# An mLSTM stage in one written order on all engines: block ends, stores, weights and roots placed a counted number of products later

## The chip, the cores and the metric

The kernel runs on one NeuronCore of a Trainium2 chip. Its time is the device time of one execution in microseconds. Three runs of the kernel before gave 2363.53 us at the median (2361.35 to 2365.49).

## The reference: what is computed

One encoder layer over 2048 tokens of width 1024, in float32. What bears on this case is the mLSTM half of the mixer, which works chunk by chunk (16 chunks of 128 tokens) for each of four heads, forward and backward in time:

```python
proj = hmix @ w_in                              # q_a, k_a, v_a, q_m, k_m, v_m, o_m, gates
qk = jax.nn.silu(centred_dwconv(jnp.concatenate([q_m, k_m], axis=-1), conv_w, conv_b))
kv_c = jnp.einsum('bchs,bchsk,bchsv->bchkv', w, kc, vc)
c_new = decay * c_st + inj * kv                 # one state per chunk, scanned over the chunks
sc = jnp.einsum('bchtd,bchsd->bchts', qc, kc) * dw
num = jnp.einsum('bchts,bchsv->bchtv', sc, vc) + inter * jnp.einsum('bchtk,bchkv->bchtv', qc, c_prev)
hout = num / jnp.maximum(jnp.abs(den), jnp.exp(-m_t))
h_m = rms_norm(h_fwd + h_bwd, g_mlstm_out)
```

The other half is banded attention (its query and key projections are made in the same stretch), followed by the output projection and a SwiGLU FFN. The output must have the reference's values to float32 accuracy; products are made of three passes with a high and a low part of each operand (`hi*hi`, `hi*lo`, `lo*hi`).

## The kernel before

The layer's input, normalised and transposed, lies in SBUF as four `hT` tiles of 512 tokens, each as a high and a low part. A projection column block of 128 columns is made by `proj_mm` (L421 to L426): for each block of 512 tokens, 8 x 3 = 24 matmuls of 128x512 (called products here) go into one PSUM bank `gps`, of which there are two. A column block is thus 4 x 24 = 96 products. Two kinds of code use it:

- `conv_tile` (L428) makes q or k of one mLSTM head: after each 24 products ACT copies the bank with the middle tap (`cacc`, L452), fixes the edges between blocks (L453 to L456), DVE adds the two side taps (L457, L458), and `finish` (L436) makes the silu of the previous block by a tanh on ACT (L439) and a product on DVE (L440), then stores it to DRAM (`qk_d`, L442).
- `qk_att` (L467) makes attention's queries and keys: a high part on ACT (`qhi`, L483), a low part on DVE (`qlo`, L484), four or eight stores.

`mlstm(h, nb, nf, last)` (L535) runs one head. Backward pass (L572 to L587): per chunk a transpose of k (`ktp`) to `kn`, `vw = w*v` on ACT, then one chunk later the matmul `kvp` and DVE's update of the state table `cb`. Forward pass (L593 to L673): `scores(cc)` makes the decay matrix `ng` (POOL L606, then two exponentials on ACT L609), `qs` (POOL L611), the matmul `sps` and DVE's `sc` (L615); one chunk later `products` makes `kvp`, the state `cf` (DVE L629), the four matmuls of `num` (L634, L636), and DVE's chain `den`, `rd`, `rd`, `rd`, `hst`, `hst` (L643 to L648), then a square with a sum on ACT (`mjk`, L650). After every fourth chunk `rsqrt` (L92) makes a root of 12 small DVE instructions and POOL scales `hst` (L653); `store` transposes it five chunks later.

Projection products fill the gaps: `fill` is a queue of generators, and `pull(n)` emits the next n products. A backward chunk pulls `nb` = 3 of them, a forward chunk `nf` = 8, and between heads 60 are pulled at once. A head therefore takes 45 + 127 products, and with the 60 between heads the projections of head h+1 are done before `mlstm(h+1)` starts.

What sets the order: PE is issued as the program is written (`tc.manual_schedule`, "hand") from here on. The other four engines' queues are in written order too ("win") during the first 252 products, where the gates are computed beside the projections of head 0; `win` is closed before `mlstm(0)`. In the mLSTM stage the order of DVE, ACT, POOL and SP is chosen by a scheduler when the program is built, from its own estimates of durations. Each engine then works through its queue in that fixed order, and one that waits holds up what stands behind it in the queue.

Loads: `load_qk` and `load_v` fetch the next block of four chunks at the block's second chunk; `load_bc` (four rows of decays, 256 KB as broadcast) is issued one chunk before its use. `proj_cols` loads and splits the weights of a column block (`whi` on ACT, `wlo` on POOL, L230, L231) when its generator begins.

Of the kernel before, what the change touches and what calls it, by code (L numbers as in the profile page):

```python
# [21 lines left out]
P = 128  # L22
# [7 lines left out]
HM = 4  # L30
# [6 lines left out]
def hybrid_layer_kernel(  # L37
# [196 lines left out]
    def proj_cols(c0):  # L234
        _, w = cols_steps(c0)
        return w
# [191 lines left out]
    def conv_tile(j, h, ws_=None):  # L428


        w = ws_[0] if ws_ else proj_cols((C_QM, C_KM)[j] + h * P)
# [5 lines left out]
        def finish(a, n):  # L437
            t = s2.tile([P, 512], F32, tag="ctanh", name="ctanh")
            act.activation(t, a, AF.Tanh)  # L439
            dve.scalar_tensor_tensor(a, t, 1.0, a, ADD, MUL)  # L440
            yield True
            sp.dma_start(qk_d[j, h, n], a)  # L442

        end = None
        for n in range(NB):
            ps = bank("g", "gps")
            for i, _ in enumerate(proj_mm(ps, w, n)):
                if end and i in (6, 14):
                    next(end, None)
                yield True  # L450
# [6 lines left out]
            dve.scalar_tensor_tensor(a[:, 1:], ps[:, :511], w0, a[:, 1:], MUL, ADD)  # L457
            dve.scalar_tensor_tensor(a[:, :511], ps[:, 1:], w2, a[:, :511], MUL, ADD)  # L458
# [5 lines left out]
        for f in (end, finish(prev, NB - 1)):  # L464
            deque(f, 0)

    def qk_att(pl, tags, j):  # L467

        w = proj_cols(C_QA + j * P)
        wait = deque()  # L470
        for n in range(NB):
            ps = bank("g", "gps")
            for i, _ in enumerate(proj_mm(ps, w, n)):
                if wait and i % 3 == 2:
                    sp.dma_start(*wait.popleft())
                yield True
            while wait:
                sp.dma_start(*wait.popleft())
# [5 lines left out]
            dve.scalar_tensor_tensor(lo, ps, s, hi.bitcast(F32), MUL, SUB)  # L484
            for i in range(2):
                rs = slice(i * 64, (i + 1) * 64)
                if j < 4:
                    wait.append((qst_d[2 * j + i, 0:64, ts], hi[rs].bitcast(F32)))
                    wait.append((qst_d[2 * j + i, 64:128, ts], lo[rs].bitcast(F32)))
                else:  # L490
                    for z in range(2):
                        wait.append((kst_d[i, 0, z * 64:(z + 1) * 64, ts], hi[rs].bitcast(F32)))
                        wait.append((kst_d[i, 1, z * 64:(z + 1) * 64, ts], lo[rs].bitcast(F32)))
        while wait:
            sp.dma_start(*wait.popleft())
# [39 lines left out]
    def mlstm(h, nb, nf, last):  # L535
# [28 lines left out]


# [3 lines left out]
        for cc in list(range(NT - 1, 0, -1)) + [0, 0]:  # L569
            tick()  # L570
            n, i = divmod(cc, 4)
            if i == 2 and n:  # L572
                blk[n - 1] = (load_qk(h, 1, n - 1), load_v(h, n - 1))
            if cc == 2:
                ahead = (load_qk(h, 0, 0), load_qk(h, 1, 0), load_v(h, 0)), load_bc(0)
# [3 lines left out]
            if len(todo) > 1 or (todo and not cc):  # L579
# [7 lines left out]
                pull(nb // 2)  # L587


        blk = {0: ahead[0]}  # L590
        out_ = {}
        bcs = {0: ahead[1]}
# [3 lines left out]
        def scores(cc):  # L596
            n, i = divmod(cc, 4)
            if cc + 1 < NT:
                bcs[cc + 1] = load_bc(cc + 1)
            if i == 2 and n + 1 < NB:  # L600
# [3 lines left out]
            bc = bcs.pop(cc)  # L604
            ng = s2.tile([P, 2, P], F32, tag="ng", name="ng")
            pool.tensor_tensor(ng, bc[:, 0:2, :], maskb, ADD)  # L606
            for d in range(2):
                rr = row(d, cc)
                act.activation(ng[:, d, :], ng[:, d, :], AF.Exp, bias=rT[:, rr:rr + 1])  # L609
# [1228 lines left out]
```

## Time and profile before

| what | time |
|---|---|
| median of three runs | 2363.53 us |
| the profiled execution | 2361.98 us |
| its span in the trace | 2360.2 us |
| PE busy in the span | 2258.3 us (96%) |
| first 252 products with the gates | about 201 to 264 us of the span |
| mLSTM stage, four heads | about 264 to 624 us |
| attention, output projection, FFN | from 624 us to the end |

Instants are microseconds from the span's start. A row of the timeline has the start, the duration, the engine, the line, the operation and what it writes and reads; in brackets the engine's idle time before it and what ended that. Matmuls overlap, so the time that one takes from the stream is the distance between two starts, not its duration. The table of windows gives busy time per engine in a stretch and the clock granted to TensorE as a share of full speed (PEclk).

### The profile page before, as it was taken

The numbers are of one execution on the slowest core, as the hardware profiler recorded it, in microseconds if no ns is written. First come the engines' busy times: TensorE is split into PE (matmuls) and PEld (weight loads), VectorE is DVE, ScalarE is ACT, GpSimd is POOL, SyncE is SP. The second block draws the span as 40 slices with busy tenths as digits, with TensorE's granted clock in tenths as the row PEclk, the third lists the DMA queues.
The fourth block names the chain that finished last, engine by engine and source line by source line (L and its number), as shares of the span: only waits on it lengthen the run. The fifth ranks groups of instructions, "written<-read, shape, count | busy, mean of one in ns | idle before, by whom it ended". The sixth has DMA issues, their size and how long they took to land.

```text
span 2360.2 us, 32454 instructions
## 1 busy us (share of the span) xinstructions
PE 2258.3 (96%) x10811; PEld 1873.2 (79%) x10811; DVE 1608.5 (68%) x2998; ACT 1061.6 (45%) x2205; POOL 1045.8 (44%) x876
## 2 busy tenths in 40 slices
PE   5998999999999999999999999899999999999998
PEld 4987777878888877777888878688888778888886
DVE  6777486676687887775656766766666645784684
ACT  3523455535487755443545434433333333233452
POOL 1004643344334433525656655465666654592020
PEclk9999999999999999999999999999999999999999
DMA  8565855477666666763343444432333273443452
GB/s 296 175 208 176 266 161 168 150 223 215 186 185 178 195 204 221 251 241 130 107 146 127 152 145 156 159 107 94 110 101 112 96 268 114 164 152 93 157 187 89
DMA packets 355515, 393.39 MB, mean 167 GB/s; under 512 B 21396, under 2 KB 253196, under 8 KB 355348
## 3 DMA queue, kind: packets, MB, share of 16 engines
q1 hardware_dynamic: 355348, 391.32, 51.4%
q8 instruction: 85, 1.39, 0.2%
q14 instruction: 82, 0.67, 0.1%
HBM read 272.06 MB, written 119.19 MB: 166 GB/s over the span
## 4 chain that ended last, share of the span: by engine, by line
PE 53%; DVE 2%; DMA 2%; issue 1%; ACT 1%; POOL 1%; SPq 0%; DVEq 0%; ACTq 0%; POOLq 0%
PE fp L56 11%; PE fp L57 11%; PE fp L58 11%; PE fo L58 6%; PE fo L56 6%; PE fo L57 6%; PE ops L56 1%; PE ops L58 1%; PE ops L57 1%; DMA al<-a_d 0%; DMA hop_d<-n 0%; DVE T L1331 0%; DMA B<-hop_d 0%; DMA a_d<-u 0%; PE trn L163 0%
## 5 line engine op out<-in xcount | busy, mean ns | idle before, releaser
L424 PE MATMUL gps<-hT,whi 128*128 128x512 f32 x1088 | 398.5, 420 | 0.0
L56 PE MATMUL fo<-w,ah 128*128 128x512 f32 x616 | 242.2, 393 | 2.6 <-ACT ah L1622 2.6
L58 PE MATMUL fo<-w,al 128*128 128x512 f32 x616 | 242.6, 394 | 0.5 <-DVE al L1623 0.5
L57 PE MATMUL fo<-w,ah 128*128 128x512 f32 x616 | 242.0, 393 | 0.0
L424 PE MATMUL gps<-hT,wlo 128*128 128x512 f32 x544 | 228.6, 420 | 0.0
L56 PE MATMUL fp<-T,S 128*128 128x512 f32 x528 | 209.4, 397 | 15.8 <-ACT u L1531 15.5
L424 PEld LDWEIGHTS gps<-hT,whi 128*128 128x128 f32 x1088 | 202.5, 191 | 24.5 <-DVE cacc L458 0.7
L57 PE MATMUL fp<-T,S 128*128 128x512 f32 x528 | 207.8, 394 | 0.8 <-DVE T L1331 0.8
L58 PE MATMUL fp<-T,S 128*128 128x512 f32 x528 | 207.5, 393 | 0.0
L1623 DVE TENSOR_TENSOR al<-al,ah 128x1024 fp32r<-128x1024 f32 x77 | 112.0, 1459 | 125.3 <-ACT ah L1622 125.1
L1366 DVE TENSOR_TENSOR A<-graw,A 128x512 fp32r<-128x512 f32 x86 | 95.7, 1119 | 123.4 <-ACT A L1365 123.2
L1366 DVE TENSOR_TENSOR S<-sf,S 128x512 fp32r<-128x512 f32 x86 | 130.1, 1551 | 59.6 <-ACT S L1365 59.5
L1622 ACT ACTIVATE ah<-al 128x1024 fp32r<-128x1024 f32 x77 | 81.6, 1060 | 189.9 <-DMA al<-a_d 189.8
L56 PEld LDWEIGHTS fo<-w,ah 128*128 128x128 f32 x616 | 116.0, 188 | 29.1 <-ACT ah L1622 3.1
L56 PE MATMUL fp<-B,A 128*128 128x512 f32 x352 | 138.1, 392 | 0.0
L58 PEld LDWEIGHTS fo<-w,al 128*128 128x128 f32 x616 | 115.9, 188 | 27.4 <-DVE al L1623 1.0
L57 PE MATMUL fp<-B,A 128*128 128x512 f32 x352 | 137.6, 391 | 0.0
L58 PE MATMUL fp<-B,A 128*128 128x512 f32 x352 | 137.6, 391 | 0.0
L57 PEld LDWEIGHTS fo<-w,ah 128*128 128x128 f32 x616 | 115.9, 188 | 26.5
L56 PEld LDWEIGHTS fp<-T,S 128*128 128x128 f32 x528 | 99.6, 189 | 40.1 <-ACT u L1531 18.1
L716 POOL TENSOR_SCALAR ap<-ap,adn 128x384 f32<-128x384 f32 (+1 forms) x128 | 73.1, 590 | 127.3 <-DVE adn L714 57.7
L1370 POOL TENSOR_TENSOR sf<-A,A22r 128x512 f32<-128x512 f32 x43 | 58.0, 1348 | 147.7 <-DMA A22r<-in_w_ffn_in_dram 116.8
(419 smaller groups left out, 6165.6 us busy)
## 6 DMA issues: line engine op xcount, KB each, us to landing
al<-a_d SPq DMA_DIRECT2D x77, 512.0 KB, 3.9
wmod<-in_w_mod_dram SPq DMA_DIRECT2D x48, 512.0 KB, 5.6
graw<-in_w_ffn_in_dram SPq DMA_DIRECT2D x43, 512.0 KB, 4.2
a_d<-ka SPq DMA_DIRECT2D x66, 256.0 KB, 4.7
bc<-bc_d SPq DMA_DIRECT2D x64, 256.0 KB, 3.7
hop_d<-n SPq DMA_DIRECT2D x56, 256.0 KB, 4.3
a_d<-u SPq DMA_DIRECT2D x55, 256.0 KB, 4.6
mqk<-qk_d SPq DMA_DIRECT2D x48, 256.0 KB, 4.1
```

What stands on the lines that cost most here:

```text
L56: pe.matmul(o, lh, rh, start=first, stop=False, skip_group_check=skip)
L57: pe.matmul(o, lh, rl, start=False, stop=False, skip_group_check=skip)
L58: pe.matmul(o, ll, rh, start=False, stop=last, skip_group_check=skip)
L424: pe.matmul(ps, w[i == 2][:, k, :], hT[n](i == 1, k), start=(k == 0 and i == 0), stop=(k == KT - 1 and i == 2))
L716: pool.tensor_scalar(self.p[g][:, :self.NK], self.p[g][:, :self.NK], dn[:, g:g + 1], 0.0, MUL, ADD)
L1366: dve.tensor_tensor(t[:, 1, :], f, t[:, 0, :].bitcast(F32), SUB)
L1370: pool.tensor_tensor(f1, a21, a22, ADD)
L1622: act.activation(ah, al.bitcast(F32), AF.Copy)
L1623: dve.tensor_tensor(al, al.bitcast(F32), ah.bitcast(F32), SUB)
```

## The change

All of it lies in the mLSTM stage. `put_soon(k, f, ...)` puts an instruction on a list, and `beat`, called after each product that `pull` emits, counts the list down and emits what is due. With it:

- a convolution block's side taps are emitted 4 products after its bank copy, the tanh 4 later, the silu product 4 after that, the store 5 later; `qlo` comes 4 products after `qhi`, the stores two products apart; the store of a normalised block 4 products after its copy; the root and POOL's scaling 5 products after the fourth chunk's square;
- weights of the next column block are loaded 6 products after the current one begins and split 48 products after (`next_cols`);
- the written order ("win") now holds for all five engines until the end of the mLSTM stage, so that no scheduler orders them there;
- loads move ahead: blocks of the backward pass at the block's first chunk, of the forward pass three chunks ahead instead of two, `bc` two chunks ahead instead of one, the next head's first block three chunks before the current head ends; block 0's keys and values, which the backward pass has loaded, are used again in the forward pass (8 loads fewer: 44 of `mqk` instead of 48, 28 of `mv` instead of 32);
- `ng` and its exponentials are made one chunk ahead (`prep`), behind `qs` of the current chunk;
- products are spread: `nb` = 4, `nf` = 10, and none between heads (60 + 159 products per head instead of 45 + 127 + 60).

No arithmetic is added or removed. The count of every instruction but the eight loads is the same, and outside the stage the order of the instructions on each engine is the same.

```diff
+    soon = []
+    def put_soon(k, f, *args):
+        soon.append([k, f, args])
+    def beat(k=1):
+        for e in soon:
+            e[0] -= k
+        due = [e for e in soon if e[0] <= 0]
+        soon[:] = [e for e in soon if e[0] > 0]
+        for _, f, args in sorted(due, key=lambda e: e[0]):
+            f(*args)
     def pull(n=1):
-        while n > 0 and fill:
-            if next(fill[0], None) is None:
+        while n > 0:
+            if not fill:
+                n -= 1
+                beat()
+            elif next(fill[0], None) is None:
                 fill.popleft()
             else:
                 n -= 1
+                beat()
...
+    ready, coming = deque(), deque()
+    def next_cols():
+        w = ready.popleft()
+        if coming and not ready:
+            g = cols_steps(coming.popleft())
+            put_soon(6, next, g)
+            put_soon(48, lambda: ready.append(next(g)))
         return w
...
+        def sides(a, ps):
+            dve.scalar_tensor_tensor(a[:, 1:], ps[:, :511], w0, a[:, 1:], MUL, ADD)
+            dve.scalar_tensor_tensor(a[:, :511], ps[:, 1:], w2, a[:, :511], MUL, ADD)
+        def finish(a, n, at):
             t = s2.tile([P, 512], F32, tag="ctanh", name="ctanh")
-            act.activation(t, a, AF.Tanh)
-            dve.scalar_tensor_tensor(a, t, 1.0, a, ADD, MUL)
-            yield True
-            sp.dma_start(qk_d[j, h, n], a)
+            put_soon(at, act.activation, t, a, AF.Tanh)
+            put_soon(at + 4, dve.scalar_tensor_tensor, a, t, 1.0, a, ADD, MUL)
+            put_soon(at + 9, sp.dma_start, qk_d[j, h, n], a)
...
-            dve.scalar_tensor_tensor(a[:, 1:], ps[:, :511], w0, a[:, 1:], MUL, ADD)
-            dve.scalar_tensor_tensor(a[:, :511], ps[:, 1:], w2, a[:, :511], MUL, ADD)
+            put_soon(4, sides, a, ps)
             if prev is not None:
-                end = finish(prev, n - 1)
-                if not ws_:
-                    deque(end, 0)
+                put_soon(7, finish, prev, n - 1, 1)
...
-            dve.scalar_tensor_tensor(lo, ps, s, hi.bitcast(F32), MUL, SUB)
+            put_soon(4, dve.scalar_tensor_tensor, lo, ps, s, hi.bitcast(F32), MUL, SUB)
...
+        def prep(cc):
+            ng = ngs[cc] = s2.tile([P, 2, P], F32, tag="ng", name="ng")
+            pool.tensor_tensor(ng, bcs[cc][:, 0:2, :], maskb, ADD)
+            for d in range(2):
+                rr = row(d, cc)
+                act.activation(ng[:, d, :], ng[:, d, :], AF.Exp, bias=rT[:, rr:rr + 1])
...
-            if i == 2 and n:
+            if i == 3 and n:
                 blk[n - 1] = (load_qk(h, 1, n - 1), load_v(h, n - 1))
             if cc == 2:
-                ahead = (load_qk(h, 0, 0), load_qk(h, 1, 0), load_v(h, 0)), load_bc(0)
+                q_first = load_qk(h, 0, 0)
+            if cc in (4, 2):
+                bcs[2 - cc // 2] = load_bc(2 - cc // 2)
...
-        blk = {0: ahead[0]}
+        blk = {0: (q_first, *blk[0])}
...
-            if cc + 1 < NT:
-                bcs[cc + 1] = load_bc(cc + 1)
-            if i == 2 and n + 1 < NB:
+            if cc + 2 < NT:
+                bcs[cc + 2] = load_bc(cc + 2)
+            if i == 1 and n + 1 < NB:
                 blk[n + 1] = (load_qk(h, 0, n + 1), load_qk(h, 1, n + 1), load_v(h, n + 1))
...
             if i == 3:
-                r = rsqrt(s2, ssq, 4, P, "mr")
-                pool.tensor_tensor(hst, hst, r.unsqueeze(2).to_broadcast([P, 4, P]), MUL)
+                put_soon(5, scaled_rows, hst, ssq)
...
+            if cc == NT - 3 and h + 1 < HM:
+                last = load_last(h + 1)
...
-    win.close()
...
-            last = load_last(h)
-            pull(60)
-        mlstm(h, 3, 8, last)
+        last = mlstm(h, 4, 10, last)
...
+    while soon:
+        beat()
+    win.close()
```

Three places show how the queues move. **ACT where head 1 begins.** `mjk` is the square of a finished chunk of head 0, `kn` and `vw` are what the first matmul `kvp` of head 1 needs, `og` belongs to a store, `ctanh`, `cacc` and `edge` to a convolution, `whi` to weights. Before:

```order
L439 ACTIVATE ctanh<-cacc 128x512
L230 ACTIVATE whi<-wraw 128x1024
L452 ACTIVATE cacc<-gps,cvb,cvw 128x512
L453 ACTIVATE edge<-gps 128x2
L554 ACTIVATE kn<-ktp 128x128
L455 ACTIVATE cacc<-edge,cacc,cvw 128x1
L456 ACTIVATE cacc<-edge,cacc,cvw 128x1
```

and in the change:

```order
L672 ACTIVATE mjk,mssq<-hst 128x128
L122 ACTIVATE ctanh<-cacc 128x512
L672 ACTIVATE mjk,mssq<-hst 128x128 x2
L568 ACTIVATE kn<-ktp 128x128
L571 ACTIVATE vw<-mv,wT 128x129
L687 ACTIVATE og<-htp,gml 128x512
L568 ACTIVATE kn<-ktp 128x128
```

Before, the last three squares of head 0 stood ten rows ahead of the first of these rows' `kn`, with three block ends (`cacc`, `edge`) between; now they stand directly in front of head 1's first `kn`, and one `og` stands between the first and the second.

**DVE in the forward pass of head 1, around a root.** `mrv`, `mry`, `mrh`, `mra` are the root's tiles, `den`, `rd`, `hst` the chain that ends a chunk, `sc` the masked scores, the `cacc` rows a convolution's side taps. Before:

```order
L104 TENSOR_TENSOR mra<-mry 128x4
L105 TENSOR_TENSOR mra<-mra,mrh 128x4
L643 COPY den<-num 128x2
L106 SCALAR_TENSOR_TENSOR mry<-mra,mry 128x4
L644 SCALAR_TENSOR_TENSOR rd<-den 128x2
L104 TENSOR_TENSOR mra<-mry 128x4
L645 TENSOR_TENSOR rd<-rd,eT 128x2
L615 SCALAR_TENSOR_TENSOR sc<-sps,ng 128x256
```

and in the change:

```order
L633 SCALAR_TENSOR_TENSOR sc<-sps,ng 128x256
L466 SCALAR_TENSOR_TENSOR cacc<-gps,cvw,cacc 128x511
L467 SCALAR_TENSOR_TENSOR cacc<-gps,cvw,cacc 128x511
L99 TENSOR_SCALAR mrv<-mssq 128x4
L101 TENSOR_SCALAR mry<-mrv 128x4
L102 TENSOR_SCALAR mrh<-mrv 128x4
L104 TENSOR_TENSOR mra<-mry 128x4
L105 TENSOR_TENSOR mra<-mra,mrh 128x4
```

The root was threaded through the chain of the next chunk; now its 12 instructions stand in one piece (three times `mra`, `mra`, `mry` in all), behind `sc` and, here, behind two side taps.

**POOL before the forward pass of head 0.** `bx`, `by`, `ts` belong to a job that prepares another weight matrix, whose last stores stand on SP's queue ahead of the loads of head 0's second block; `wlo` is a split of projection weights. Before:

```order
L231 TENSOR_TENSOR wlo<-wraw,whi 128x1024
L862 TENSOR_TENSOR bx<-bx,gb 128x512
L864 TENSOR_TENSOR by<-by,gb 128x512
L875 TENSOR_TENSOR ts<-bx 128x256
L875 TENSOR_TENSOR ts<-by,bx 128x256
L875 TENSOR_TENSOR ts<-by,ts 128x256 x2
```

and in the change:

```order
L891 TENSOR_TENSOR bx<-bx,gb 128x512
L893 TENSOR_TENSOR by<-by,gb 128x512
L904 TENSOR_TENSOR ts<-bx 128x256
L904 TENSOR_TENSOR ts<-by,bx 128x256
L904 TENSOR_TENSOR ts<-by,ts 128x256 x2
L248 TENSOR_TENSOR wlo<-wraw,whi 128x1024
```

The split has moved behind the last `ts`, and the stores that wait for `ts` come due earlier by its length.

More of the change, by code (lines that the diff above doesn't have):

```diff
@@ L483, in qk_att @@
             act.activation(hi, ps, AF.Copy, scale=s)
[L484 removed]
+            put_soon(4, dve.scalar_tensor_tensor, lo, ps, s, hi.bitcast(F32), MUL, SUB)
+            at = 6
             for i in range(2):
                 rs = slice(i * 64, (i + 1) * 64)
[L487 to L495, printed above, removed]
+                for y, t in enumerate((hi, lo)):
+                    for z in range(1 if j < 4 else 2):
+                        o = qst_d[2 * j + i, y * 64:(y + 1) * 64, ts] if j < 4 else kst_d[i, y, z * 64:(z + 1) * 64, ts]
+                        at += 2
+                        put_soon(at, sp.dma_start, o, t[rs].bitcast(F32))
     oslots = deque()
@@ L673, in mlstm @@
             todo = new
+        return last
     def att_loads(bi, kv):
```

63 lines of the change are left out of this document (25 added, 38 removed).

## The prediction

> **What bounds the kernel now.** I read the page first, then the windows of the four forward passes, the timeline of PE, and the waits.
>
> ```profile
> span 2360.2 us, 32454 instructions
> PE 2258.3 (96%) x10811; PEld 1873.2 (79%) x10811; DVE 1608.5 (68%) x2998; ACT 1061.6 (45%) x2205; POOL 1045.8 (44%) x876
> ```
>
> PE is busy for 96% of the span, so a change of order can only win waits of PE. A page's share hides where they are. The next four rows are the forward passes of heads 0 to 3 (stretch, then its length, then busy time of PE, PEld, DVE, ACT, POOL):
>
> ```profile
> 286.30:337.60 51.30, 49.06 (x296) 41.46 (x295) 40.57 (x152) 29.26 (x94) 26.88 (x31) 1.00 0.64 192
> 377.30:428.20 50.90, 48.22 (x295) 41.48 (x294) 42.33 (x152) 28.37 (x93) 24.24 (x30) 1.00 0.52 160
> 464.60:515.80 51.20, 47.68 (x295) 41.45 (x294) 39.84 (x148) 25.71 (x82) 26.93 (x31) 1.00 0.75 212
> 551.50:600.90 49.40, 47.29 (x296) 41.61 (x294) 38.54 (x147) 22.12 (x74) 24.02 (x31) 1.00 0.66 192
> ```
>
> DVE is busy for 40 of 51 us. The waits of 264 to 625 us say what it and PE wait for (total, times, longest):
>
> ```profile
> DVE mrv L99 <- ACT mjk L650: 13.4, 14, 2.6
> DVE cacc L457 <- ACT edge L453: 13.3, 10, 3.9
> POOL ng L606 <- DMA bc<-bc_d: 34.5, 13, 9.4
> PEld sps L613 <- DVE sc L615: 9.3, 11, 2.1
> ```
>
> DVE stands 26.7 us (13.4 + 13.3) behind an ACT result that its queue has asked for too early, with PE's `sc` and `cf` behind it. So the stage is PE's, delayed by DVE's queue. How much, the stream's starts tell: the first `kvp`, the first `sps` and the last `sps` of each head, and one steady chunk.
>
> ```profile
> 267.46 0.49 PE L562 MATMUL kvp<-vw,kn 128*128 128x129 f32 x2 [0.63 <-ACT kn L554]
> 286.29 0.49 PE L613 MATMUL sps<-mqk 128*128 128x128 f32 x2
> 337.56 0.49 PE L613 MATMUL sps<-mqk 128*128 128x128 f32 x2
> 359.58 0.38 PE L562 MATMUL kvp<-vw,kn 128*128 128x129 f32 x2
> 377.26 0.40 PE L613 MATMUL sps<-mqk 128*128 128x128 f32 x2
> 428.22 0.49 PE L613 MATMUL sps<-mqk 128*128 128x128 f32 x2
> 449.81 0.38 PE L562 MATMUL kvp<-vw,kn 128*128 128x129 f32 x2
> 464.55 0.40 PE L613 MATMUL sps<-mqk 128*128 128x128 f32 x2
> 515.82 0.49 PE L613 MATMUL sps<-mqk 128*128 128x128 f32 x2 [1.76 <-DVE sc L615]
> 536.23 0.38 PE L562 MATMUL kvp<-vw,kn 128*128 128x129 f32 x2
> 551.46 0.38 PE L613 MATMUL sps<-mqk 128*128 128x128 f32 x2
> 565.50 0.38 PE L613 MATMUL sps<-mqk 128*128 128x128 f32 x2
> 568.70 0.38 PE L613 MATMUL sps<-mqk 128*128 128x128 f32 x2
> 600.86 0.49 PE L613 MATMUL sps<-mqk 128*128 128x128 f32 x2 [1.16 <-DVE sc L615]
> ```
>
> A steady forward chunk takes 568.70 - 565.50 = 3.20 us. From first to last `sps` are 15 steps; 15 x 3.20 = 48.0 us, less about 1.1 because the first two steps have no or fewer `num` and `kvp` matmuls and two steps carry a store's transposes (my estimate from the same stream): 46.9 us. The four passes took 51.27, 50.96, 51.27 and 49.40, so **15.3 us of waits in the forward passes**. The backward passes (first `kvp` to first `sps`) took 18.83, 17.68, 14.74 and 15.23: over the shortest, **7.5 us**. The boundaries (last `sps` to the next first `kvp`, with 60 products in them) took 22.02, 21.59, 20.41: over the shortest, **2.8 us**. Together 25.6 us are to be had at most.
>
> **The change part by part.** Products are moved, not removed: 4 heads x (15 + 30) more inside the passes, 3 x 60 fewer at the boundaries. One costs
>
> ```profile
> 254.66 0.62 PE L424 MATMUL gps<-hT,whi 128*128 128x512 f32 x2
> 255.34 0.39 PE L424 MATMUL gps<-hT,whi 128*128 128x512 f32 x1
> ```
>
> (255.34 - 254.66) / 3 = 0.23 us, so a forward chunk grows to 3.20 + 2 x 0.23 = 3.66 us, a boundary shrinks by 13.7, and the sum is zero. The eight loads fewer (256 KB each) and the earlier ones cost SP issue time alone; SP is on no path of PE except at the two waits below. That leaves three terms.
>
> *Forward passes.* DVE's work in a chunk, and the pieces that the change places anew:
>
> ```profile
> 489.61 0.34 DVE L629 SCALAR_TENSOR_TENSOR cf<-cf,dec,kvp 128x129 f32<-128x129 f32 x1
> 492.25 0.34 DVE L629 SCALAR_TENSOR_TENSOR cf<-cf,dec,kvp 128x129 f32<-128x129 f32 x1
> L458 DVE SCALAR_TENSOR_TENSOR cacc<-gps,cvw,cacc 128x511 f32<-128x511 f32 x20 | 15.0, 749 | 4.1 <-ACT cacc L456 3.4
> L440 DVE SCALAR_TENSOR_TENSOR cacc<-ctanh,cacc 128x512 f32<-128x512 f32 x21 | 16.7, 799 | 0.2 <-ACT ctanh L439 0.2
> L645 DVE TENSOR_TENSOR rd<-rd,eT x64: 147/162/2303, 291.6 to 605.8; 128x2 f32<-128x2 f32 x64
> L105 DVE TENSOR_TENSOR mra<-mra,mrh 128x4 f32<-128x4 f32 x48 | 11.0, 230 | 0.8
> ```
>
> A convolution block costs DVE 2 x 0.75 + 0.80 = 2.30 us per 24 products, 0.96 for ten. Ten products give DVE 15 x 2 x 0.096 = 2.9 us more work in a pass that grows by 15 x 0.46 = 6.9. From 42.33 busy of 46.9 needed by PE (90%) it goes to 45.2 of 53.8 (84%); the root no longer threaded through the chain costs more, since each of its 12 dependent instructions then waits for the one before (12 x 0.2 = 2.4 us in one piece, by L105, against about half of that when threaded): 4 x 1.2 = 4.8, so 50.0 of 53.8 (93%). What ends: the waits on `mjk` (root 5 products later), on `edge` and `qhi` (4 products, 0.9 us and more, later), and the chain from `bc` through `ng` to `sc`, now a chunk ahead. What stays: ACT's square still waits for DVE's `hst` in front of the next `cacc`, and side taps emitted early in a chunk can still wait for it. I bound the waits left by 1 us a pass (PE's small hitches in a steady stretch) and by all 15.3. Nearer the low end, since heads 2 and 3 carry `qk_att` with a third of the DVE work: 2 x 2 + 2 x 0.75 = 5.5 left, **9.8 us won**.
>
> *Backward passes.* Head 0's excess of 4.1 us is one late load and what follows it:
>
> ```profile
> 272.15 0.33 PE L552 MATMUL ktp<-ident,mqk 128*128 128x128 f32 x1 [1.92 <-DMA mqk<-qk_d]
> 272.80:276.10 3.30, 3.30 (x12) 2.73 (x11) 1.80 (x4) 2.14 (x8) 0.00 (x0) 0.50 1.00 341
> 624.01 0.36 PE L700 MATMUL as<-ak,aq 128*128 128x256 f32 x1 [2.13 <-DMA ak<-kst_d]
> 624.40:627.70 3.30, 3.30 (x12) 2.85 (x12) 2.03 (x9) 1.86 (x7) 0.00 (x0) 0.50 0.94 261
> L231 POOL TENSOR_TENSOR wlo<-wraw,whi x10: 2377/2394/2405, 293.9 to 614.6; 128x1024 fp32r<-128x1024 f32 x10
> ```
>
> The load stands on SP behind stores that wait for POOL; POOL's `wlo` (2.4 us) goes behind them, and four products a chunk give 4 x 0.23 = 0.9 us more. Both waits at the load should go, with the 3.3 us at half clock behind it (1.7 us lost). Against that ACT, no longer ordered by the scheduler, puts a block end ahead of `kn`:
>
> ```profile
> L452 ACT ACTIVATE cacc<-gps,cvb,cvw 128x512 f32<-128x512 f32 x22 | 16.9, 767 | 5.7 <-PE gps L424 5.7
> L650 ACT ACTIVATE mjk<-hst 128x128 bf16<-128x128 f32 x64 | 19.2, 300 | 21.7 <-DVE hst L648 14.9 <-DVE rd L644 2.8 <-DVE mry L106 2.2
> L557 ACT ACTIVATE vw<-mv,wT 128x129 f32<-128x129 f32 x120 | 46.3, 397 | 20.7 <-PE kvp L562 8.8 <-DMA mv<-vaug_d 8.5 <-PE ktp L552 1.8
> ```
>
> That is 0.77 and three small ones, 1.3 to 1.7 us, against about 0.85 us of slack in a step: 0 to 0.85 a block, I take 0.5; 60 products are 2.5 blocks, three heads have convolutions there: 3.8, and 0.8 for the fourth head's `qhi` and for weight splits, which I cannot price closer. 7.5 - 4.6 = **2.9 us won**.
>
> *Boundaries.* The 60 products were the cover under which the last chunk of a head ended. Now its square `mjk` stands in front of `kn`, and `kvp` behind that. From the last chunk's step PE has 2.5 us of other work up to the first `kvp` (six products 1.4, four `num` groups and two transposes 1.1). DVE needs two chains of about 2.1 us (the rows from 489.61 to 492.25, less `sc` and `cf`), then ACT `mjk` 0.3 to 0.5, `kn` 0.3, `vw` 0.4: 5.2. So 1.6 to 2.8 us a boundary; I take 2.0, by three 6.0, in place of 2.8: **3.2 us lost**.
>
> A pause has a second price. After the pauses of 1.92 and 2.13 us TensorE ran 3.3 us at 0.50 of its clock. I add 1.5 us for three boundaries near that length, one time in two or three. The Trainium skill ("TensorE: Matmul & The Clock Gate", Part 1) has the clock fall only after an idle window of about 3.4 us; by that rule the boundaries would cost no clock and the sum be 1.5 us better, but here pauses of 2 us were enough, and I go by the rows.
>
> The wait for `ak` at 624 stays: its load follows the same last stores on SP. The stretch before 264 us I cost at 0, bounds 1 us either way. Sum: 9.8 + 2.9 - 3.2 - 1.5 = 8.0 us. The profiled execution took 2361.98 us (span 2360.2 and 1.8 around it), so 2354.0; the median of the runs lies 1.5 us above it. I predict **2355 us** (rounded down from 2355.5).
>
> **The rivals.** *DVE becomes the bound* (slower). In heads 0 and 1 the forward chunk needs 2.64 us for chain, `sc` and `cf` (489.61 to 492.25), 0.96 for ten products, 0.62 for the root: 4.2 us by single durations, against 3.66 for PE. The sums of durations overstate (they give 4.0 before, where 3.4 ran), but an instruction on 128x2 took up to 2.3 us (L645), as long as POOL's `wlo`, and a root in one piece offers POOL twelve such victims. If a chunk takes X, 32 chunks cost 32 (X - 3.66) less the 8.5 us of waits these two passes have now; with the rest of the sum (5.4 won in heads 2 and 3, 2.9 won, 4.7 lost) the kernel is slower from X = 4.04 on, and at 4.2 it ends at 2369. For it: the numbers above. Against: DVE's busy rows, 84 to 93%. The skill ("SBUF — State Buffer", Who interferes with whom) states that a DVE instruction with two SBUF inputs and a GpSimd one that reads SBUF lock each other out for a whole instruction; that agrees with the 2.3 us.
>
> *The waits only move* (no change). Forward passes win half (7.7), the boundaries pay 2.8 and a half-clock window of 1.7 each (13.5 in place of 2.8): 7.7 + 2.9 - 10.7 = 0; 2363.
>
> *Nearly all waits go* (faster still): 22 of the 25.6 us, boundaries hidden by products behind `kvp`: 2341. Against it stands ACT's queue at the boundary.
>
> *Loads are asked for earlier but land no earlier*, since SP's queue is in order and its stores now wait for later instructions: head 0 keeps its 4.1 us: 2359.
>
> **How the numbers follow.** Forecast 0.50, nearly all waits go 0.13, loads no earlier 0.05, waits only move 0.17, DVE the bound 0.15. About 0.2% (4.7 us) is what a measurement can tell from no change. The first two are faster, and half of the third; some of the forecast's lower end is not: faster 0.63, same 0.21, slower 0.16. The forecast's own range is 2348 to 2360; to leave out two in ten it reaches 2343 to 2367.
>
> **What would show it.** Right: the waits of DVE on `mjk` and `edge` fall well below 26.7 us, `sps` waits little for `sc`, steady chunks of 3.66 us, no `mqk` wait near 272 us and no half clock there, a wait of `kvp` at about 2 us where heads 1, 2 and 3 begin. Wrong: forward chunks of 4 us and more in heads 0 and 1 with DVE busy over 95% (DVE bound), half-clock windows at the boundaries (waits only move), or a boundary without a pause.

## The result, and the profile after

The changed kernel took 2395.62 us at the median of four runs (2392.65 to 2402.82); the kernel before, with a fourth run beside them, 2362.44 us (2354.04 to 2365.49). The measured ratio is 1.0162 with a 95% interval of 1.0138 to 1.0185: slower by 1.6%, where 0.3% faster was forecast. (The ratios here and below are those of the measurement; they are not the quotients of the medians, which would be 1.0140 here.) The profiled execution of the change took 2397.67 us. Its page:

```profile
span 2395.9 us, 32402 instructions
PE 2264.7 (95%) x10811; PEld 1873.6 (78%) x10811; DVE 1633.3 (68%) x2998; ACT 1058.9 (44%) x2205; POOL 1044.4 (44%) x876
```

The page shows next to nothing: 95% in place of 96%. The windows of the four forward passes (first to last `sps`; stretch, length, then busy time of PE, PEld, DVE, ACT, POOL, and the granted clock) show it:

```profile
284.10:350.70 66.60, 57.55 (x325) 48.23 (x324) 49.18 (x161) 30.15 (x98) 27.45 (x32) 0.97 0.42 134
378.20:447.80 69.60, 56.67 (x325) 46.70 (x323) 50.70 (x162) 30.51 (x101) 30.71 (x37) 1.00 0.41 125
478.00:536.80 58.80, 55.59 (x326) 47.00 (x324) 45.37 (x154) 25.20 (x87) 25.82 (x33) 1.00 0.71 211
566.20:628.70 62.50, 55.79 (x325) 47.04 (x324) 44.74 (x149) 23.59 (x79) 28.85 (x36) 1.00 0.59 165
```

At the prediction's 3.66 us a chunk a pass needs 15 x 3.66 - 1.1 = 53.8 us. These took 257.5, which is 42 us too much; before it was 15.3. DVE is busy for 72 to 77% of the passes, so on average it is not short of time. The waits of 264 to 665 us (total, times, longest) say what happens:

```profile
ACT mjk L672 <- DVE hst L670: 141.7, 56, 6.2
PEld sps L631 <- DVE sc L633: 25.7, 22, 3.2
DVE cacc L466 <- ACT edge L480: 16.0, 12, 2.7
DVE qlo L122 <- ACT qhi L500: 14.7, 11, 2.5
DVE cacc L122 <- ACT ctanh L122: 12.6, 9, 2.5
```

ACT stands 141.7 us at its square (14.9 before), DVE stands 43 us (16.0 + 14.7 + 12.6) for pieces that ACT has queued behind that square, and PE's `sps` waits for DVE's `sc`. A timeline of head 1 shows one round after the other:

```profile
388.11 0.35 DVE L670 SCALAR_TENSOR_TENSOR hst<-num,rd,hst 128x128 f32<-128x128 f32 x1
388.49 0.31 ACT L672 ACTIVATE mjk<-hst 128x128 bf16<-128x128 f32 x1 [3.80 <-DVE hst L670]
388.80 0.39 ACT L571 ACTIVATE vw<-mv,wT 128x129 f32<-128x129 f32 x1
389.10 0.68 ACT L587 ACTIVATE ng<-ng,rT 128x128 f32<-128x128 f32 x2
389.68 0.76 ACT L479 ACTIVATE cacc<-gps,cvb,cvw 128x512 f32<-128x512 f32 x1
390.35 0.15 ACT L480 ACTIVATE edge<-gps 128x2 f32<-128x2 f32 x1
390.53 0.75 DVE L466 SCALAR_TENSOR_TENSOR cacc<-gps,cvw,cacc 128x511 f32<-128x511 f32 x1 [1.48 <-ACT edge L480]
393.21 0.35 DVE L670 SCALAR_TENSOR_TENSOR hst<-num,rd,hst 128x128 f32<-128x128 f32 x1
393.48 0.41 DVE L633 SCALAR_TENSOR_TENSOR sc<-sps,ng 128x256 f32<-128x256 f32 x1
393.60 0.31 ACT L672 ACTIVATE mjk<-hst 128x128 bf16<-128x128 f32 x1 [2.40 <-DVE hst L670]
393.95 0.49 PE L631 MATMUL sps<-mqk 128*128 128x128 f32 x2 [0.44 <-DVE sc L633]
394.79 0.61 ACT L122 ACTIVATE ctanh<-cacc 128x512 f32<-128x512 f32 x1
395.44 0.69 DVE L122 SCALAR_TENSOR_TENSOR cacc<-ctanh,cacc 128x512 f32<-128x512 f32 x1 [1.54 <-ACT ctanh L122]
396.54 0.46 PE L576 MATMUL kvp<-vw,kn 128*128 128x129 f32 x2 [0.47 <-DVE den L665]
397.91 0.31 ACT L672 ACTIVATE mjk<-hst 128x128 bf16<-128x128 f32 x1 [2.51 <-DVE hst L670]
```

The square waits for `hst`; behind it ACT does `vw`, two exponentials, `cacc`, `edge`; DVE has been waiting 1.48 us for `edge`, then does the taps and the chain up to the next `hst`; and the square waits for that. A round takes 393.60 - 388.49 = 5.11 us, the next (by way of `ctanh`) 4.31, against 3.66 for the ten products of a chunk. In these rounds neither engine is busy all the time; each stands in front of the other (called the ring below).

Not every step is such a round. The four passes have 60 steps from one `sps` to the next; undisturbed, a step takes 3.66 us, the first two of a pass 1.95 and 3.44, one with a store's transposes 4.1. In 16 steps DVE waits over 0.3 us for `edge`, `ctanh` or `qhi`, and they are 18.3 us too long together. Eleven others are 20.6 us too long, and in them DVE hardly pauses (less than 0.75 us each). One loses 2.4 us to the first `ng` of head 1, and the other 32 lose 0.9 us in all. The longest step of head 1, from 402.09 to 409.21, is of the second kind:

```profile
402.69 0.16 DVE L99 TENSOR_SCALAR mrv<-mssq 128x4 f32<-128x4 f32 x1
404.67 0.16 DVE L106 SCALAR_TENSOR_TENSOR mry<-mra,mry 128x4 f32<-128x4 f32 x1
405.01 1.55 DVE L122 SCALAR_TENSOR_TENSOR cacc<-ctanh,cacc 128x512 f32<-128x512 f32 x1
408.74 0.41 DVE L633 SCALAR_TENSOR_TENSOR sc<-sps,ng 128x256 f32<-128x256 f32 x1
409.21 0.49 PE L631 MATMUL sps<-mqk 128*128 128x128 f32 x2 [1.93 <-DVE sc L633]
```

DVE works through the root in one piece (first and last instruction shown), a product that takes 1.55 us here and 0.69 above, and the chain, and only then comes to `sc`. On average DVE has time; in such a step it has not.

By stage, from the starts of the matmuls in the two profiles (their spans differ by 35.7 us, their last matmuls by 36.0):

| part | forecast | measured |
|---|---|---|
| forward passes, waits | -9.8 | +27.0 (42.3 in place of 15.3) |
| backward passes | -2.9 | -3.9 (3.6 in place of 7.5) |
| three boundaries, with the clock | +4.7 | +7.6 (10.4 in place of 2.8) |
| up to the first `kvp` | 0 | -2.9 |
| last `sps` to attention's first matmul | 0 | +2.3 |
| attention to the last matmul | 0 | +5.9 |

The last row lies behind the change. In the kernels below, which alter nothing there either, that part took 1726 to 1738 us from profile to profile (1727.6 before); what sets it was not looked into.

### The profile page after: what moved, and what is told of

Same layout as the page of the kernel before. It is cut to its first block, busy times and chain, and to the rows that moved or that the text cites. A ratio compares the mean times of both kernels' runs of the same rounds, so it can differ in the third digit from the quotient of the medians.

```text
span 2395.9 us, 32402 instructions
## 1 busy us (share of the span) xinstructions
PE 2264.7 (95%) x10811; PEld 1873.6 (78%) x10811; DVE 1633.3 (68%) x2998; ACT 1058.9 (44%) x2205; POOL 1044.4 (44%) x876
## 4 chain that ended last, share of the span: by engine, by line
PE 67%; DVE 12%; DMA 7%; ACT 4%; issue 4%; POOL 2%; SPq 1%; ACTq 0%; DVEq 0%; POOLq 0%
PE fp L56 11%; PE fp L57 11%; PE fp L58 11%; PE gps L452 7%; PE fo L58 5%; PE fo L57 5%; PE fo L56 5%; PE atp L752 1%; PE ops L56 1%; PE ops L58 1%; PE ops L57 1%; DMA vst_d<-vs 1%; DVE macc L365 1%; DMA al<-a_d 1%; DVE rd L666 1%
## 5 line engine op out<-in xcount | busy, mean ns | idle before, releaser
L1392 DVE TENSOR_TENSOR A<-graw,A 128x512 fp32r<-128x512 f32 x86 | 101.4, 1187 | 121.8 <-ACT A L1391 121.7
```

Of the source, the lines that this page charges most:

```text
L1392: dve.tensor_tensor(t[:, 1, :], f, t[:, 0, :].bitcast(F32), SUB)
```

## The experiments

**One part at a time.** Theory A: the written order makes ACT and DVE wait for each other in turn. Its rivals: the even spread of the products, or DVE's work. Four kernels ran beside the kernel before (2355.66 us there).

The square later:

```diff
-            act.activation(jk, hst[:, i, :], AF.Square, accum_out=ssq[:, i:i + 1])
+            put_soon(8, squared, jk, hst[:, i, :], ssq[:, i:i + 1])
...
-                put_soon(5, scaled_rows, hst, ssq)
+                put_soon(12, scaled_rows, hst, ssq)
```

> The changed kernel with one edit: ScalarE's square of a chunk's output (mjk) stands 8 products later in the written order, and the root with the scaling of the four rows 12 products after the block instead of 5. Nothing else moves. Theory A (the written order makes ScalarE and VectorE wait for each other in turn: ScalarE stands 141.7 us in 56 waits of mjk on VectorE's hst, and the block ends behind it make VectorE and then PE late): those waits go to below 20 us, the forward passes fall from 66.6/69.7/58.8/62.5 us to some 55 to 58 each, and the time falls by 20 to 32 us, to 2364 to 2376. Rival B (VectorE has too much work in a chunk, or the even spread of 10 products itself is what costs): the waits of mjk go, the forward passes stay within 2 us of what they were, time 2392 to 2398. Rival C (the wait only moves to the next thing that ScalarE or VectorE stands at): half of it, 2380 to 2388.

The order of the four engines back to the scheduler, all else of the change kept:

```diff
     assert min(due) > 1 << 20
+    win.close()
...
-    win.close()
     assert not fill and not later
```

> The changed kernel, but in the mLSTM stage the scheduler orders VectorE, ScalarE, GpSimd and SyncE again, as it does in the kernel before; the loads further ahead, the later block ends and the spread of 4 and 10 products stay. Theory A (the set order is what costs): the mjk waits on hst fall from 141.7 us to near the kernel before's level, forward passes at 55 to 60 us, time 2355 to 2372. Rival B (spread, loads or lack of the 60 products at the boundary cost, not the order): time 2385 to 2398.

The spread alone, in the kernel before:

```diff
             last = load_last(h)
-            pull(60)
-        mlstm(h, 3, 8, last)
+        mlstm(h, 4, 10, last)
```

> The kernel before with one part of the change: 4 and 10 products per chunk in place of 3 and 8, and no run of 60 products between heads. The order stays the scheduler's. Theory A (the spread is harmless): forward chunks of 3.66 us with waits like before (15 us in all), boundaries lose their cover of 13.7 us each but no work: time 2355 to 2372. Rival B (the spread is what costs: boundaries bare, with load_last's loads asked for only there): boundaries wait 3 to 8 us each for mqk, backward passes late too, time 2375 to 2395.

The change without the spread:

```diff
+            pull(60)
-        last = mlstm(h, 4, 10, last)
+        last = mlstm(h, 3, 8, last)
```

> The changed kernel with the old spread: 3 and 8 products per chunk and 60 products between heads; set order, block ends by count, loads ahead stay. Theory A (the set order costs in the forward passes, whatever the spread): mjk still waits over 100 us for hst, the forward passes stand 8 to 15 us above the 48 us that they need at 3.20 us a chunk, only the boundaries get 2 to 5 us each back: time 2380 to 2396. Rival B (the spread costs): forward passes at 50 to 52 us, time 2355 to 2366.

Measured, with the four forward passes and their excess over what the products need (46.9 us with 8, 53.8 with 10):

| kernel | us | ratio to before | passes | excess |
|---|---|---|---|---|
| square later | 2371.22 | 1.0070 [1.0055, 1.0085] | 59.0, 64.4, 56.0, 56.2 | 20 |
| scheduler | 2358.67 | 1.0000 [0.9983, 1.0017] | 55.2, 54.5, 56.1, 58.4 | 9 |
| spread alone | 2357.99 | 1.0016 [1.0005, 1.0027] | 57.0, 55.8, 56.6, 59.7 | 14 |
| change without spread | 2414.00 | 1.0242 [1.0216, 1.0268] | 65.5, 69.9, 61.6, 55.2 | 65 |

One moved ScalarE instruction per chunk, and the root that needs it, bring the change from 1.62% over the kernel before to 0.70%, some 22 us; the share of the root's own move was not separated. The waits fall as theory A said, though `mjk` not below 20 us, and head 1's pass (64.4 us) not to its 55 to 58:

```profile
ACT ng L587 <- POOL ng L584: 96.6, 49, 4.6
ACT mjk L679 <- DVE hst L670: 26.4, 21, 4.7
DVE cacc L466 <- ACT edge L480: 6.9, 12, 1.5
```

The spread and the loads are not what costs 1.6%: with the scheduler's order they stand at 1.0000, and the spread alone at 1.0016. And the last kernel missed its expectation on the telling side. Its passes in heads 0 and 1, with 8 products a chunk:

```profile
274.70:340.20 65.50, 52.77 (x295) 44.43 (x296) 49.63 (x158) 27.80 (x93) 26.50 (x34) 0.94 0.43 137
376.70:446.70 70.00, 51.56 (x296) 42.71 (x295) 49.58 (x159) 29.46 (x98) 31.04 (x37) 0.98 0.38 121
```

65.5 and 70.0 us with 8 products, 66.6 and 69.6 with 10. PE's work does not set the length of these two passes; the queues of ACT and DVE do, though a step that neither disturbs still takes PE's 3.20 us there (290.42 to 293.62). So the 60 products that go back to each boundary are paid on top, and it is the slowest of all.

**What is left, and the other side of the ring.** Four kernels beside the kernel before (2356.11 us). In the first, `prep(cc + 1)` stands ahead of `qs` in `scores`, with the square later:

> The kernel with the square 8 products later, and one more edit: GpSimd's sum for the next chunk's gates (ng) stands in front of its product for this chunk (qs) instead of behind it. In that kernel ScalarE stood 96.6 us in 49 waits for ng, since GpSimd's qs waits for the buffer that the products (num) of the chunk before release. Theory A (the same fault once more: an engine waits with other work queued behind): the waits of ScalarE on ng fall below 40 us, heads 0 and 1 lose 2 to 8 us each in the forward pass (59.0 and 64.4 us there), time 2355 to 2366 beside 2371. Rival B (ScalarE has slack there and only VectorE's work counts): the waits fall, the time stays within 3 us of 2371.

In the second the root is also cut in four (three instructions, and a turn of three after 2, 4 and 6 more products each):

> As the run with ng first, and the root of four chunks (12 small VectorE operations in one piece, 2.1 us in a row at 395.8 to 397.9 us in the profile of the kernel with the square later) in four pieces, two products apart. Theory A (what is left is VectorE's queue coming late by a burst): the waits of PE on sc and den that follow a root go, 1 to 1.5 us in 3 of every 4 roots, 12 to 20 us in 16 roots at most: time 2345 to 2358. Rival B (the pieces stand just as much in front of the rest, since VectorE has little room in heads 0 and 1): the same within 3 us as with ng first.

The third leaves the square where the change has it and puts DVE's pieces off:

```diff
-            put_soon(4, sides, a, ps)
+            put_soon(10, sides, a, ps)
...
-            put_soon(at + 4, dve.scalar_tensor_tensor, a, t, 1.0, a, ADD, MUL)
+            put_soon(at + 10, dve.scalar_tensor_tensor, a, t, 1.0, a, ADD, MUL)
...
-            put_soon(4, dve.scalar_tensor_tensor, lo, ps, s, hi.bitcast(F32), MUL, SUB)
+            put_soon(10, dve.scalar_tensor_tensor, lo, ps, s, hi.bitcast(F32), MUL, SUB)
```

> The changed kernel with the square where the change has it, at once, and VectorE's parts of a block end 6 products later (side taps and low halves 10 instead of 4 after the block, the product with tanh 10 after the tanh). It takes VectorE's waits on ScalarE away and leaves ScalarE's wait on VectorE. Theory A (the two wait for each other, and either side of the ring opens it): the waits of VectorE on edge, qhi and ctanh (43 us in the changed kernel) fall below 15, the forward passes to 55 to 60 us, time 2362 to 2376, though ScalarE still waits some 100 us for hst. Rival B (only ScalarE's early stop counts): over 2388.

The fourth has all of them:

> The run with the root in pieces, and VectorE's parts of a block end 6 products later as well. Theory A: the forward passes come within 2 us of 55 each, time 2338 to 2352, faster than the kernel before. Rival B (VectorE's own work, stretched by GpSimd, sets the rest): forward passes of heads 0 and 1 stay at 58 or more, time 2352 to 2362.

Measured, in this order: 2364.62 (1.0026 [1.0011, 1.0041]), 2371.30 (1.0058 [1.0038, 1.0077]), 2370.39 (1.0060 [1.0046, 1.0075]) and 2368.04 (1.0046 [1.0025, 1.0068]).

DVE's pieces later are worth what the square later is, 1.0% or 24 us. In that kernel's stretch of 262 to 625 us ACT still stands at its square, but DVE hardly comes too early any more for what lies behind:

```profile
ACT mjk L672 <- DVE hst L670: 117.9, 51, 5.4
DVE cacc L466 <- ACT edge L480: 2.2, 3, 1.5
```

Its passes (60.2, 65.5, 57.1 and 59.4 us) still stand 27 us over their need, and head 1's is well over the 55 to 60 expected. `ng` first gave 0.4% on top of the square later (1.0070 to 1.0026). The time is in theory A's range, its mechanism is not shown: ACT's waits on `ng` fell from 96.6 to 74.6 us only, not below 40, and the passes of heads 0 and 1 lost 2.1 and 0.7 us, not 2 to 8 each. The root in pieces gave nothing: the forward passes are 231.2 us in place of 232.3, and the kernel is 7 us slower, which neither of its theories had; its waits at the boundaries, of the kind told below, are 2.5 us longer, and the rest lies behind the stage in these profiles and stays unexplained. All three together did not come to the 2338 to 2352 expected, though head 3's pass reached 53.8 us, exactly what its products need. (The profiled execution of this kernel took 2357.15 us, 11 us less than its median.) The timeline of that kernel shows what stood in the way where head 1's pass begins:

```profile
363.68 2.39 POOL L248 TENSOR_TENSOR wlo<-wraw,whi 128x1024 fp32r<-128x1024 f32 x1 [13.81 <-ACT whi L247]
366.02 1.41 POOL L584 TENSOR_TENSOR ng<-bc,maskb 128x256 f32<-128x256 f32 x2
368.05 0.49 PE L631 MATMUL sps<-mqk 128*128 128x128 f32 x2 [2.22 <-DVE sc L633]
```

A weight split of 2.39 us on POOL stands ahead of the first chunk's `ng`, and `sc` and `sps` wait for that. Likewise the transposes of a head's last block waited 1.5, 2.9 and 1.3 us for rows that are now scaled later, and `num` of the last chunk 1.4 us in two heads.

**A mended order.** The next kernel has the square later, `ng` first and DVE's pieces later, the root in one piece again, and takes these waits away where the order makes them: the first `ng` two chunks earlier, the last block's store three steps later (so the loop behind the last head runs nine times, not six), four products in front of the last chunk's.

```diff
-            if cc in (4, 2):
-                bcs[2 - cc // 2] = load_bc(2 - cc // 2)
+            if cc in (6, 4):
+                bcs[3 - cc // 2] = load_bc(3 - cc // 2)
+            if cc == 2:
+                prep(0)
...
-                later.append([5, lambda: store(n, hst)])
+                later.append([5 if n < NB - 1 else 8, lambda: store(n, hst)])
...
                 pull(nf - 3)
+            else:
+                pull(4)
```

> The changed kernel with every wait that the runs so far left on PE's path taken away in the written order: square 8 products later, ng in front of qs, VectorE's parts of a block end 6 products later, the gates' sum of a head's first chunk two chunks earlier (its scores' result waited 2.2 us for it behind wlo in three heads), the store of a head's last block three steps later (its transposes waited 1.5 to 2.9 us for the scaled rows), and 4 products in front of the last chunk's products (num waited 1.4 us there in three heads). In the profile of the run with all three these waits are 6.6, 6.7 and 4.1 us. Theory A (each is time of PE's path): 2368 less some 13 to 17, so 2350 to 2356, at or just under the kernel before. Rival B (they move on): 2360 or more.

> As the mended kernel, but VectorE's parts of a block end stand where the change has them (4 after the block, 4 after the tanh). If the distance of 4 products (0.9 us) is enough once ScalarE no longer stands at mjk (theory A): within 4 us of the mended kernel. If VectorE still comes to ScalarE's edge, qhi and ctanh too early (rival B): 4 to 10 us slower, in heads 0 and 1.

> The mended kernel, but with the scheduler ordering the four engines in the mLSTM stage. If a good written order is worth what the scheduler's is (theory A): within 4 us of the mended kernel. If a written order can beat it: mended 5 us or more under this one.

Beside them the square at 4 products instead of 8 in the otherwise unmended change:

> As the run with the square 8 products later, but 4 (root 8). The output hst of a chunk is ready some 2.2 us after the last of its products, 4 products are 0.9 us. Theory A (ScalarE's stop is what costs, so the time follows how long it stops): mjk waits for hst about half as long as with the change, time between 2376 and 2388. Rival B (any place behind the chunk's end will do): 2368 to 2373, as with 8.

Measured beside 2356.43 us of the kernel before: mended 2356.47 (1.0002 [0.9990, 1.0015]); with DVE's pieces early 2357.69 (0.9995 [0.9983, 1.0007]); mended with the scheduler 2349.85 (0.9973 [0.9960, 0.9986]); square at 4 2371.53 (1.0060 [1.0042, 1.0079]). The mended kernel came to the edge of theory A's range, but its profile does not show why. In the profile of the run with all three the 2.2 us before a first `sc` stand in head 1 alone, not in three heads, and PE's waits of the three kinds, 11.9 us there, are still 7.1 us in the mended kernel, 5.7 of them now before the last head's `htp`. From the first `kvp` to attention's first matmul the two profiles differ by 2.3 us (359.1 and 356.9), the medians by 11.6. So a written order with these faults mended equals the scheduler's of the kernel before and is 6.6 us behind the scheduler's on the same mended program, which was in neither theory's numbers. Four products are distance enough for DVE once ACT doesn't stop, as far as the time shows. And by the time the square at 4 is as good as at 8, against theory A's number: at 4 it stands behind the next chunk's exponentials, which wait for POOL's `ng` anyway (109.6 us in all there), and `hst` is done when ACT comes to it (mjk waits 20.9 us, less than the 26.4 at 8). Here the place in the queue counts, not the number of products.

**Whose order it is.** Two kernels hand one queue of the changed kernel back to the scheduler and keep the other three written, and a third looks at a wait left in the best kernel.

```diff
     assert min(due) > 1 << 20
+    win.close()
+    win.enter_context(tc.manual_schedule(engines={getattr(mybir.EngineType, e) for e in ("DVE", "Pool", "SP")}))
```

> The changed kernel, but in the mLSTM stage only ScalarE's queue is ordered by the scheduler again; VectorE, GpSimd and SyncE keep the written order. Theory A1 (the fault is where ScalarE's own queue has the square): mjk's waits for hst fall from 141.7 us to under 40, time 2358 to 2373, as with the square 8 products later (2371) or better. Theory A2 (the written order of VectorE is at fault as much): 2378 or more.

The other names `("Activation", "Pool", "SP")`:

> The changed kernel, but only VectorE's queue is ordered by the scheduler; ScalarE, GpSimd and SyncE keep the written order, the square in front of the next chunk's work among it. Theory A1 (ScalarE's queue alone is at fault): mjk still waits over 100 us for hst, time 2380 to 2396. Theory A2 (the ring opens from VectorE's side too, as it did with VectorE's parts 6 products later): 2360 to 2376.

> The mended kernel with the scheduler (2349.85 us), and the last head with 9 products a chunk and none in front of its last chunk, which keeps 20 products (4.6 us) for the steps behind it: there PE stood 5.05 us before htp at 600.1 us, waiting for the scaled rows of the last block, with no product left. Theory A (a wait with no work to cover it is time): 3 to 5 us less, 2345 to 2347. Rival B (the products only come before the wait instead of behind it, and the end of the stage is set by their number): within 2 us of 2349.85.

Measured beside 2358.24: ScalarE free 2361.44 (1.0027 [1.0013, 1.0042]), VectorE free 2358.29 (1.0011 [0.9993, 1.0029]). Either one opens the ring; it was made by the pair, not by one queue. With VectorE free ACT's square still waits much, and DVE little (262 to 625 us):

```profile
ACT mjk L672 <- DVE hst L670: 78.2, 47, 5.6
DVE cacc L466 <- ACT edge L480: 7.1, 15, 1.3
```

Opening the ring is not all that the order needs. The steps of the passes, sorted as above (us too long, number of steps):

| kernel | passes' excess | DVE waits for `edge`, `ctanh`, `qhi` | DVE does not pause |
|---|---|---|---|
| the change | 42 | 18.3 (16) | 20.6 (11) |
| square later | 20 | 3.2 (3) | 12.1 (12) |
| DVE's pieces later | 27 | 0 | 22.0 (14) |
| ScalarE free | 22 | 0 | 21.0 (13) |
| VectorE free | 10 | 2.4 (1) | 1.6 (4) |
| scheduler | 9 | 5.5 (3) | 1.6 (2) |

The steps in which DVE does not pause go when the scheduler orders DVE's queue, and stay in good part in the other kernels. What in DVE's written order makes them is not separated; cutting the root in pieces alone did not help. ScalarE free and VectorE free are as close as they are in time because VectorE free loses at the boundaries (30.6 us for the three, against 21.7) most of what it wins in the passes.

The third kernel took 2349.79 us (0.9969 [0.9956, 0.9982]), the same as the 2349.85 without its edit: the rival was right. The wait before `htp` is gone there, but attention's first matmul, at 610.23 us without a wait before, now waits for its load and starts at the same time:

```profile
598.92 0.60 PE L689 MATMUL htp<-ident,hst 128*128 128x128 f32 x4
610.21 0.35 PE L735 MATMUL as<-ak,aq 128*128 128x256 f32 x1 [2.48 <-DMA ak<-kst_d]
```

Both mended kernels with the scheduler beat the kernel before, by 0.3%, and the change by 1.9%.

## Why the prediction was wrong

*What bounds the kernel before.* Right: PE, held up by DVE's queue where it comes to an ACT result too early.

*The forward term.* This is the step that failed: 5.5 us of waits left were forecast, 42.3 were. It failed in two places. One is the sentence "What stays: ACT's square still waits for DVE's `hst` in front of the next `cacc`, and side taps emitted early in a chunk can still wait for it", which stands for 18.3 us. I had seen both arrows and priced each as a small wait, when together they are a loop with a round of its own. Its length can be read from durations: the square with its sum, `vw`, two exponentials, `cacc` and `edge` take ACT 2.0 us (388.49 to 390.50), the two taps and the chain take DVE 3.1 (390.53 to 393.60): 5.1 us against 3.66. I checked that DVE's work fits into a pass (throughput), not whether the two engines' queues can overlap (latency). The other place is that check itself, "50.0 of 53.8 (93%)". The busy time came out (49.2 and 50.7 us in heads 0 and 1), but it is a sum over a pass, and a chunk whose step has a root and a block's end in it has more work for DVE than the step is long. The term has nothing for that; the steps in which DVE does not pause lost 20.6 us. My upper bound of 15.3 us was no bound either: it supposed that an order can be no worse than the scheduler's.

*That the waits on `edge` and `qhi` end, since they come 4 products later.* They rose, with `ctanh` from 24 to 43 us. The waits of the root on `mjk` did end (1.4 us in place of 13.4). Four products are enough when ACT is free (the kernel with DVE's pieces early: 2357.69) and not when it stands at the square.

*Backward passes.* Right in size: 3.9 us won, 2.9 forecast, in part by luck. The forecast left about 1.3 us in each of heads 0 to 2 and 0.8 in head 3; measured are 1.4, 0.4, 0.1 and 1.7. The late load did not vanish, though. It moved to the head's first transpose, outside the passes:

```profile
262.38 0.48 PE L566 MATMUL ktp<-ident,mqk 128*128 128x128 f32 x1 [5.05 <-DMA mqk<-qk_d]
```

The half clock behind it (0.50 from 261.6 to 268.4 us) reaches into head 0's pass. The stretch up to the first `kvp` still ended 2.9 us earlier; in the other kernels' profiles it ended at 257.1 to 265.2 us, so this shows no effect of the change.

*Boundaries.* The step was right: `kn` behind the last squares. At head 1 it costs what I took, 2.0 us:

```profile
359.04 0.33 PE L566 MATMUL ktp<-ident,mqk 128*128 128x128 f32 x1 [1.87 <-ACT kn L568]
456.10:459.60 3.50, 3.28 (x12) 2.32 (x12) 2.29 (x9) 1.91 (x9) 0.00 (x0) 0.51 0.67 201
```

With the spread alone the three boundaries lose 6.5 us over the 6.7 that each needs; I had 6.0. In the changed kernel they lose 10.4, since the ring makes the last chunk of head 1 late (PE waits 1.83 us for its `sc` and 1.21 us for `den`) and half clock follows there (second row).

*The rivals.* "DVE becomes the bound" foretold slower, with forward chunks over 4 us in heads 0 and 1. They came, 4.4 and 4.6 on average, but with DVE busy 74 and 73% of the pass, not over 95%. Step by step it names about half of the loss: in the eleven steps without a pause DVE is busy for 89 to 93%, and they stay when the ring is opened from DVE's side (DVE is then busy for 51.8 of the 60.2 us of head 0's pass). "The waits only move" and "loads no earlier" each hold for a piece, the load at 262 us among them. That a set order could be worse than the one it replaces, as a mechanism with its own price, was not among them.

## What to carry to other kernels

When two in-order queues feed each other inside one loop, add up the round trip (from an engine's stop, through all that stands behind it, to the other engine and back) and compare it with the time of a step; busy shares and sums of work do not show it. Then add up each engine's work in the fullest step, not in the average one: a burst that exceeds its step is paid as well. A result that nobody needs soon, like a square for a later root, belongs behind what another engine waits for; here moving that square and its root gave back over 20 us. The written order took several such mends to be worth as much as the scheduler's.

## What the runs showed of the hardware

A DVE instruction on 128x4 took 2.33 us in the mended kernel with the scheduler, to the end of a POOL split that had started beside it, where others of its kind took 0.16:

```profile
596.17 2.34 POOL L248 TENSOR_TENSOR wlo<-wraw,whi 128x1024 fp32r<-128x1024 f32 x1 [8.48 <-ACT whi L247]
596.20 2.33 DVE L104 TENSOR_TENSOR mra<-mry 128x4 f32<-128x4 f32 x1
598.57 0.16 DVE L105 TENSOR_TENSOR mra<-mra,mrh 128x4 f32<-128x4 f32 x1
```

The profile has the whole of it as the instruction's own duration, so such time counts as busy. That the two lock each other out is what the Trainium skill states ("SBUF — State Buffer", Who interferes with whom), and these rows agree.

The stretches at half clock last 3.4 or 6.8 us, and their starts lie on a grid: in the changed kernel's trace 346.9 and 456.1 us are 32 steps of 3.41 us apart, and 261.6 and 630.2 us lie 25 steps before the one and 51 behind the other. A pause of 2.53 us ends inside one; one of 1.87 us (before 359.04) does not, and one of 2.89 us does not either:

```profile
347.53 0.77 PE L576 MATMUL kvp<-vw,kn 128*128 128x129 f32 x2 [2.53 <-DVE den L665]
346.90:350.30 3.40, 2.77 (x11) 2.62 (x12) 3.12 (x10) 0.15 (x1) 2.41 (x3) 0.50 0.00 0
429.91 0.49 PE L631 MATMUL sps<-mqk 128*128 128x128 f32 x2 [2.89 <-DVE sc L633]
```

On that grid the pause of 2.89 us falls in two steps, 1.8 and 1.1 us, while 1.9 us of the 2.53 lie in one. What decides does not come out of these traces: further on in the same one, a step with 1.58 us idle (790.66 to 794.07) is followed by half clock, and the step with the 1.87 us is not. The Trainium skill ("TensorE: Matmul & The Clock Gate", Part 1) speaks of at least one idle window of about 3.4 us; the step agrees, a whole idle one was not needed here.
